# Precomputed weight sums in DRAM scratch, and gate products on VectorE, in a one-core block kernel

## The chip, the cores and the metric

One core of one Trainium2 chip runs the whole kernel. The metric is the device time of one execution in microseconds: 713.98 us is the median of three runs (713.1 to 714.77).

## The reference

One layer of a sequence model with x of 512 positions by 1024 features, all float32:

```python
h = rms_norm(x, norm_mix_g)
cb, cc, cin, q, k, v, f_logit, g_logit = split(h @ w_in)
y_conv = (cb * causal_dwconv(cc * cin, conv_mix_w)) @ w_out_conv
o = forgetting_attention(q, k, v, log_sigmoid(f_logit + b_f))     # 8 heads of 64, causal
y_attn = o @ w_out_attn
g_conv, g_attn = split(sigmoid(g_logit + b_gate))
x = x + (g_conv * y_conv + g_attn * y_attn) @ w_o
h = rms_norm(x, norm_ffn_g)
a, b = split(causal_dwconv(h @ w_up, conv_ffn_w))                 # 2 x 2816 wide
x = x + (silu(a) * b) @ w_down
return rms_norm(x, norm_f_g)
```

## The kernel before

Everything is kept transposed: 128 features on the partitions, 512 positions along a row. Every product is made of three matmuls. A float32 weight is split into a high part (`wh`, rounded to float32r by ScalarE) and a low part (`wl`, the rest, one subtraction on VectorE), the activations likewise, and high by high, low by high and high by low are summed in PSUM (`mm3`, in halves of 256 positions).

Weights stream from DRAM in chunks of 128 x 1024 in a fixed list `stream`. `load` issues the DMA of a chunk on SP's queue into a raw buffer, `split` makes `wh` and `wl` of it (two buffers each), `chunk` hands them to the matmuls. `load` runs up to `LOOK = 7` chunks ahead (`AHEAD = 3` during attention), as far as raw buffers are free.

The stages in order: v projection; attention, with the conv, q and k projections filled in between its heads (32 score units; each unit's softmax product `pp` is scaled on GpSimd and transposed three units later); the gate stage, j = 0 to 7, with for each j the two gates of a 128-feature block, then the chunk `mix` (y_conv into PSUM tile `yc`, y_attn into `ya`), then the merge into `mh` and `ml`; w_o (`wo`); up projection with 12 of 22 blocks (two `up` chunks each), first down projection, up projection of the other 10, second down projection; the last down blocks and the final norm.

Some products of 2 x 2 blocks are made with seven block products instead of eight: the gates of j = 3 to 7 (`gate_pair`) and most of the down projection (`down`). A step covers two such sets, and its weights are 14 blocks of 128 x 128: six plain ones (chunk `P`) and eight that are sums (chunk `F`). The table `wst` holds a step in DRAM. Two of four kinds of sum are made while loading: SP loads four blocks into the F buffer, GpSimd issues a second DMA that adds four blocks to them, then two GpSimd additions of 128 x 256 (L182 and L183, in `forms`) make the other four from these and P. P chunks and ordinary ones share four raw buffers, F chunks have four of their own (`NRAW`).

In `gate_pair`, VectorE assembles the two gates `a` (`ga`) and `b` (`gb`) from four PSUM banks, and GpSimd multiplies both by the norm factor `rb1` (L812, L813). ScalarE takes the sigmoid. VectorE multiplies by `yc` and `ya`, GpSimd adds the two (L850), ScalarE and VectorE split the sum.

For j = 1 and 2 the gates are ordinary products (PSUM tile `p_g`), and beside them x is loaded again in quarters (`xq`, DMAs on GpSimd's queue) and turned into the sums that the seven-product form needs (`x_forms`: tiles `tq`, `txh`, `txl`). In the up stage GpSimd multiplies silu(a) by b (`ge` for even j, `go` for odd j, the last of a phase on VectorE); `gh` and `gl` hold the split result for `down`, whose PSUM tiles are `dn`.

`keep` fixes an instruction's place on its engine; the rest is ordered by a scheduler. An engine's queue runs in order: what waits at its head holds all behind it.

Of the kernel before, what the change touches and what calls it, by code (L numbers as in the profile page):

```python
# [13 lines left out]
P = 128  # L14
# [9 lines left out]
EPS = 1e-6  # L24
AHEAD = 3
LOOK = 7
NRAW = {"raw": AHEAD + 1, "rf": 4}
NWARM = 7
NPP = 4
NCT = 5  # L30
# [30 lines left out]
def block_kernel(ctx, tc, xT, vecs, wv, win, wmix, wo, wup, wst, wdp, outT):  # L61
# [10 lines left out]
    def keep(ins):  # L72
        return tc.keep_in_program_order(ins)
# [38 lines left out]
    early = qk_i[0] + qk_i[1]  # L112
    late = conv_i[0] + qk_i[2] + conv_i[1] + qk_i[3] + conv_i[2] + conv_i[3] + [20, 28]

    def double(n):
# [25 lines left out]
    rfp = []  # L141
    later = []
    held = dict.fromkeys(NRAW, 0)
    stage = {"add": 0, "sum": 0}

    def after_split():

# [2 lines left out]
            st.enter_context(tc.issue_after(ins))  # L150
        return st

    def tag_of(k):
        return "rf" if stream[k][0][0] == "F" else "raw"

    def load(upto):
        for k in range(len(raws), min(upto, len(stream) - 1) + 1):
            nm, src, ncol = stream[k]
            tag = tag_of(k)
            if held[tag] == NRAW[tag] or tag == "rf" and not rfp:  # L160
                return
            held[tag] += 1
            raw = (rfp[0] if tag == "rf" else wp).tile([P, D], F32, tag=tag, name=f"raw_{nm}", bufs=NRAW[tag])
            if k == 0:

                keep(nc.scalar.dma_start(raw[:, :VW], src[:, :VW]))
                keep(nc.sync.dma_start(raw[:, VW:ncol], src[:, VW:]))
            elif tag == "rf":
                keep(nc.sync.dma_start(raw[:, : 4 * P], src[:, : 4 * P]))
# [7 lines left out]
    def forms(k):  # L177
        while stage["sum"] <= min(k + 3, stage["add"] - 1):
            a = stage["sum"]
            if tag_of(a) == "rf":  # L180
                f, p = (raws[x].rearrange("p (a b) -> p a b", b=P) for x in (a, a - 1))
                keep(nc.gpsimd.tensor_add(f[:, 4:6], f[:, 0:4:2], p[:, 1:6:3]))  # L182
                keep(nc.gpsimd.tensor_add(f[:, 6:8], f[:, 4:6], p[:, 2:6:3]))  # L183
            stage["sum"] += 1
        while stage["add"] < len(raws):
            a = stage["add"]
            if tag_of(a) == "rf":
                keep(nc.gpsimd.dma_start(raws[a][:, : 4 * P], stream[a][1][:, 4 * P :], accum_op=ALU.add))
            stage["add"] += 1

    def run_later(k, us):

# [17 lines left out]
    def split(hl=None):  # L210

        k = len(parts)
        if k == len(stream):
            return
        nm, _, ncol = stream[k]
        load(k + (LOOK if k >= gs0 else AHEAD))
        forms(k)
        if hl is None:
            hl = []
            for x in "hl":  # L220
                if k == 0:
                    wp.tile([P, PADW[x]], F32, tag=f"pad{x}", name=f"pad_{x}")
                hl.append(wp.tile([P, D], F32R, tag=f"w{x}", name=f"w{x}_{nm}", bufs=2)[:, :ncol])
        hi, lo = hl
        raw = raws[k]
        if k == 0:
            for cs in (slice(0, VW), slice(VW, S + H)):
                keep(nc.vector.tensor_copy(hi[:, cs], raw[:, cs]))
        else:
            ins = nc.scalar.activation(hi, raw, AF.Copy)  # L230
            order["hi"] = ins.ins
            if k < KB:
                keep(ins)
        ins = nc.vector.tensor_sub(lo, raw, hi.bitcast(F32))  # L234
        order["lo"] = ins.ins
        if k < KB:
            keep(ins)
        held[tag_of(k)] -= 1
        assert tag_of(k) == "raw" or stage["sum"] > k
        parts.append((hi, lo))  # L240
        run_later(k, {"u": 1.7, "P": 1.6, "F": 0.75}.get(nm[0], 3.5))

# [50 lines left out]
    )  # L293

    def place_of(f, s_):
        c = 3 * s_ + f if f < 3 else 2 * s_ + f - 3 if f < 5 else 4 + s_ + 2 * (f - 5)
        return slice(c * P, (c + 1) * P)

    def pair(ns, form, banks):
# [428 lines left out]
    for i in range(n + LA):  # L728
        if i < n:
            scores(*units[i])  # L730
        take = 1 if i < n + LA - 1 else len(fill)
# [14 lines left out]
    rfp.append(gxp)  # L746
# [76 lines left out]
    for j in range(KB):  # L823
        gs = []
        if j == 0:
            x_load(0)
            x_load(1)
            evac_gate(0, gs)(gp[0])
            evac_gate(8, gs)(gp[1])
        elif j < GS:  # L830
            for c, ev in enumerate((evac_gate(j, gs), evac_gate(8 + j, gs))):
                run_all(proj(20 + 8 * c + j, f"g{c}{j}", ev, acc))
                q = 2 * j - 2 + c
                x_forms(q)
# [12 lines left out]
        a, b = gs  # L847
        nc.vector.tensor_mul(a, a, yc)
        nc.vector.tensor_mul(b, b, ya)
        nc.gpsimd.tensor_add(a, a, b)  # L850
# [4 lines left out]
    rfp.clear()  # L855
# [68 lines left out]

    fp = ctx.enter_context(tc.tile_pool(name="fp", bufs=1))
    fp.tile([P, PADL], F32, tag="pad", name="pad_f")
    rfp.append(fp)

# [275 lines left out]
def _layout(i):  # L1204
# [41 lines left out]
    wup = blocks(i["w_up"][0])  # L1246
    wup = np.stack([wup[:NP], wup[NP:]], axis=1).reshape(2 * NP, P, D)
    wdn = blocks(i["w_down"][0]).reshape(KB, P, NP, P)
    wst = []
    for d in STEPS[0] + STEPS[1]:  # L1250
        def pick(*which):
            return [wdn[2 * i + m, :, 2 * q + k] for i, q in d for m, k in which]

        w = pick((1, 1), (0, 0), (0, 1)) + pick((1, 0), (1, 0)) + pick((1, 1), (0, 0))
        wst.append(np.concatenate(w, axis=1))
    for j in range(GS, KB):
        for d in range(2):
            w = []
            for which in (((1, 1), (0, 0), (0, 1)), None, ((1, 1), (0, 0))):
                for q in (2 * d, 2 * d + 1):  # L1260
                    for m, k in which or ((1, 0), (1, 0)):
                        w.append(win[20 + 8 * m + j][:, (2 * q + k) * P : (2 * q + k + 1) * P])
# [38 lines left out]
```

## Time and profile before

| | |
|---|---|
| median of three runs | 713.98 us (713.1 to 714.77) |
| profiled execution | 711.97 us, span 710.2 us |
| mean granted TensorE clock | 0.996 |
| GpSimd additions of 128 x 256 at L182 | 27, mean 1281 ns |
| low parts of F chunks (`wl_F`, L234) | 27, mean 1500 ns |
| low parts of up chunks (`wl_up`, L234) | 44, mean 1223 ns |
| DMAs on GpSimd's queue | 11.31 MB, 8.3% of 16 DMA engines over the span |
| DMAs on SP's queue | 70.65 MB, 31.7% |

The profile shows one execution on the chip. PE is TensorE's matmuls, PEld its weight loads, DVE is VectorE, ACT ScalarE, POOL GpSimd, SP the queue that issues most DMAs. A timeline row begins with its start and its duration in us; a name left of the arrow is the tile written, names right of it are read; in brackets stands how long the engine was idle before it, and what ended that. A row of waits has the waiting line, the awaited one, and then the total in us, the number of waits and the longest.

### The profile page before, as it was taken

Reading aid. Unit: us, or ns where it says so; the run is one execution under the profiler, and the core shown is the slowest. Engines: PE = TensorE matmul, PEld = TensorE weight load, DVE = VectorE, ACT = ScalarE, POOL = GpSimd, SP = SyncE. Lnnn points to the kernel's source line nnn. Section 1 sums busy time; section 2 is a strip of 40 time slices with the busy share of each in tenths; the row PEclk is TensorE's granted clock in tenths of the full one; section 3 lists DMA queues with packets and bytes.
Section 4 is the critical chain, followed back from the end, with each engine's and each line's share of the span. In section 5 each row is a group of like instructions: output and inputs, shape, how many; then the busy total and the mean of one; then the engine's idle time right before and its main releaser. Section 6 shows DMA issues by size and latency. Waiting matters only on the chain. (4 is left out here: it accounts for less than half of the span.)

```text
span 710.2 us, 14598 instructions
## 1 busy us (share of the span) xinstructions
PE 694.5 (98%) x6017; PEld 690.6 (97%) x6017; DVE 506.7 (71%) x772; ACT 340.4 (48%) x538; POOL 225.3 (32%) x234
## 2 busy tenths in 40 slices
PE   8999999999999999999999999999999999999995
PEld 8999999999999999999999999999999999999995
DVE  6677777766477788744377777779885678878953
ACT  6665645555465443344254444445443345444542
POOL 4124433322134677343301101136740110116202
PEclk9999999999999999999999999999999999999998
DMA  8513222222355655462323322357863332256303
GB/s 255 167 63 112 69 66 86 63 87 61 120 178 136 177 134 141 142 205 93 90 90 98 112 90 90 115 137 173 216 151 103 94 115 90 90 143 148 93 27 120
DMA packets 31491, 84.11 MB, mean 118 GB/s; under 512 B 3744, under 2 KB 6432, under 8 KB 31424
## 3 DMA queue, kind: packets, MB, share of 16 engines
q1 hardware_dynamic: 24736, 70.65, 31.7%
q0 software_dynamic: 5424, 11.31, 8.3%
q10 hardware_dynamic: 1264, 1.22, 0.5%
q8 instruction: 47, 0.77, 0.5%
q14 instruction: 20, 0.16, 0.1%
HBM read 81.00 MB, written 2.10 MB: 117 GB/s over the span
## 5 line engine op out<-in xcount | busy, mean ns | idle before, releaser
L264 PE MATMUL p_up<-x1h,wh_up 128*128 128x256 f32 x536 | 104.5, 276 | 0.0
L264 PE MATMUL p_up<-x1l,wh_up 128*128 128x256 f32 x536 | 104.4, 276 | 0.0
L264 PE MATMUL p_up<-x1h,wl_up 128*128 128x256 f32 x536 | 104.4, 276 | 0.0
L230 ACT ACTIVATE wh_up<-raw_up 128x1024 fp32r<-128x1024 f32 x44 | 46.7, 1060 | 89.1 <-PE p_up L264 68.8
L264 PEld LDWEIGHTS p_up<-x1h,wh_up 128*128 128x128 f32 x536 | 80.7, 188 | 0.0
L264 PEld LDWEIGHTS p_up<-x1l,wh_up 128*128 128x128 f32 x536 | 80.7, 188 | 0.0
L264 PEld LDWEIGHTS p_up<-x1h,wl_up 128*128 128x128 f32 x536 | 80.7, 188 | 0.0
L234 DVE TENSOR_TENSOR wl_up<-raw_up,wh_up 128x1024 fp32r<-128x1024 f32 x44 | 53.8, 1223 | 20.6 <-ACT wh_up L230 20.6
L264 PE MATMUL p_in<-xgh,wh_in 128*128 128x256 f32 x288 | 56.9, 279 | 1.0 <-ACT wh_in L230 1.0
L960 POOL TENSOR_TENSOR ge<-fu,fu 128x512 f32<-128x512 f32 x11 | 17.1, 1554 | 126.3 <-DVE fu L538 113.4
L264 PE MATMUL p_in<-xgh,wl_in 128*128 128x256 f32 x288 | 56.5, 277 | 0.0
L264 PE MATMUL p_in<-xgl,wh_in 128*128 128x256 f32 x288 | 56.4, 277 | 0.0
L230 ACT ACTIVATE wh_F<-raw_F 128x1024 fp32r<-128x1024 f32 x27 | 28.7, 1065 | 52.6 <-PE ya L264 24.7
L234 DVE TENSOR_TENSOR wl_F<-raw_F,wh_F 128x1024 fp32r<-128x1024 f32 x27 | 40.5, 1500 | 18.2 <-ACT wh_F L230 18.1
L947 DVE TENSOR_TENSOR fz<-p_up,rb_n 128x512 f32<-128x512 f32 x44 | 30.3, 690 | 30.1 <-PE p_up L264 30.1
L264 PEld LDWEIGHTS p_in<-xgh,wh_in 128*128 128x128 f32 x288 | 44.7, 188 | 1.9 <-ACT wh_in L230 1.2
L264 PEld LDWEIGHTS p_in<-xgl,wh_in 128*128 128x128 f32 x288 | 43.6, 188 | 0.0
L264 PEld LDWEIGHTS p_in<-xgh,wl_in 128*128 128x128 f32 x288 | 43.5, 188 | 0.0
L182 POOL TENSOR_TENSOR raw_F<-raw_F,raw_P 128x256 f32<-128x256 f32 x27 | 34.6, 1281 | 18.4 <-DMA raw_F<-in_wst_dram 18.4
L282 PE MATMUL p_up<-x1h,wh_up 128*128 128x256 f32 x168 | 40.3, 277 | 0.0
L282 PE MATMUL p_up<-x1l,wh_up 128*128 128x256 f32 x168 | 40.2, 276 | 0.0
L234 DVE TENSOR_TENSOR wl_in<-raw_in,wh_in 128x1024 fp32r<-128x1024 f32 x26 | 33.1, 1275 | 6.7 <-ACT wh_in L230 6.3
(309 smaller groups left out, 2119.4 us busy)
## 6 DMA issues: line engine op xcount, KB each, us to landing
raw_up<-in_wup_dram SPq DMA_DIRECT2D x44, 512.0 KB, 3.6
raw_in<-in_win_dram SPq DMA_DIRECT2D x26, 512.0 KB, 3.5
raw_P<-in_wst_dram SPq DMA_DIRECT2D x27, 384.0 KB, 3.6
raw_F<-in_wst_dram SPq DMA_DIRECT2D x27, 256.0 KB, 3.5
raw_F<-in_wst_dram POOLq DMA_DIRECT2D x27, 256.0 KB, 4.5
raw_mix<-in_wmix_dram SPq DMA_DIRECT2D x8, 512.0 KB, 4.1
raw_wo<-in_wo_dram SPq DMA_DIRECT2D x8, 512.0 KB, 3.6
xq<-in_xT_dram POOLq DMA_DIRECT2D x8, 256.0 KB, 3.9
```

Source lines behind the costliest of these rows:

```text
L182: keep(nc.gpsimd.tensor_add(f[:, 4:6], f[:, 0:4:2], p[:, 1:6:3]))
L230: ins = nc.scalar.activation(hi, raw, AF.Copy)
L234: ins = nc.vector.tensor_sub(lo, raw, hi.bitcast(F32))
L264: keep(nc.tensor.matmul(out[:, cs], w, x[:, cs], start=start and i == 0 and c == 0, stop=stop and i == 2 and c == len(cut) - 1,))
L282: keep(nc.tensor.matmul(out, wl if x == 1 else wh, xl if x == 2 else xh, start=opens and bk not in seen, stop=closes and bk not in left,))
L947: nc.vector.tensor_mul(z, p, rb2)
L960: keep(nc.gpsimd.tensor_mul(ge, a.rearrange(halves_of, h=2), b.rearrange(halves_of, h=2)))
```

## The change

The table `wst` keeps ten blocks a step. The sums of F are made in DRAM scratch (pool `dsp`, tiles `sum0` to `sum13`, two steps a tile, the last one step) by six DMAs a tile: copy four blocks, add four blocks; copy two of the sums on, add two blocks; copy those on, add two blocks. Copies go to SP's queue, adds (`accum_op`) to GpSimd's. The list `todo` holds all 84, two tiles' lists interleaved; `tick` issues the next one: once for each attention score unit, and afterwards at each split of an ordinary chunk (`in`, `mix`, `wo`, `up`) and of every second F. F is then loaded like any chunk, from the scratch. All chunks share five raw buffers; the F buffers and `forms` are gone.

The products with `rb1` and the sum of the two gated terms move to VectorE, for all eight j. The yc matmuls take all high parts of the weight first and its low part last. Nothing else of the arithmetic changes.

```diff
-NRAW = {"raw": AHEAD + 1, "rf": 4}
+NRAW = 5
+    def group(i):
+        ns = groups[i]
+        t = dsp.tile([P, len(ns), D], F32, tag=f"sum{i}", name=f"sum{i}")
...
+        return [
+            copy(f(0, 4), w(6, 10)),
+            add(f(0, 4), w(0, 4)),
+            copy(f(4, 6), f(0, 2)),
+            add(f(4, 6), w(2, 4)),
+            copy(f(6, 8), f(4, 6)),
+            add(f(6, 8), w(4, 6)),
+        ]
+    for i0, i1 in ((0, ngate), (ngate, len(groups))):
+        for i in range(i0, i1, 2):
+            todo += [op for ops in zip(*(group(x) for x in range(i, min(i + 2, i1)))) for op in ops]
+    def tick():
+        if todo:
+            todo.pop(0)()
     def double(n):
-        return [(f"P{n}", wst[n, :, : 6 * P], 6 * P), (f"F{n}", wst[n, :, 6 * P :], D)]
+        return [(f"P{n}", wst[n, :, : 6 * P], 6 * P), (f"F{n}", sums[n], D)]
...
-                keep(nc.gpsimd.tensor_add(f[:, 4:6], f[:, 0:4:2], p[:, 1:6:3]))
-                keep(nc.gpsimd.tensor_add(f[:, 6:8], f[:, 4:6], p[:, 2:6:3]))
...
-                keep(nc.gpsimd.dma_start(raws[a][:, : 4 * P], stream[a][1][:, 4 * P :], accum_op=ALU.add))
...
-        forms(k)
+        if k >= gs0 and (nm[0] in "imwu" or nm[0] == "F" and int(nm[1:]) % 2):
+            tick()
...
-            nc.gpsimd.tensor_mul(a, a, rb1)
-            nc.gpsimd.tensor_mul(b, b, rb1)
+            nc.vector.tensor_mul(a, a, rb1)
+            nc.vector.tensor_mul(b, b, rb1)
...
-        for pp, hh, ll, o in ((yc, ych, ycl, 0), (ya, oth, otl, 4)):
-            for k in range(4):
-                ks = slice((o + k) * P, (o + k + 1) * P)
-                mm3(pp, wh[:, ks], wl[:, ks], hh[:, k, :], ll[:, k, :], k == 0, k == 3)
+        passes([
+            (yc[:, cs], 0, wh[:, k * P : (k + 1) * P], wl[:, k * P : (k + 1) * P], ych[:, k, cs], ycl[:, k, cs],
+             True, True)
+            for k in range(4) for cs in halves
+        ], 8)
+        for k in range(4):
+            ks = slice((4 + k) * P, (5 + k) * P)
+            mm3(ya, wh[:, ks], wl[:, ks], oth[:, k, :], otl[:, k, :], k == 0, k == 3)
...
-        nc.gpsimd.tensor_add(a, a, b)
+        nc.vector.tensor_add(a, a, b)
```

How it stands on the engines. VectorE, one gate step (j = 5 there), from the assembly of the gates to the merged result's low part; before:

```order
L807 TENSOR_TENSOR gz_3337<-gs_3224,gz_3337 128x256
L808 TENSOR_TENSOR gb_3338<-gs_3222,gz_3337 128x512
L234 TENSOR_TENSOR wl_F_3403<-raw_F_3135,wh_F_3402 128x1024
L848 TENSOR_TENSOR ga_3336<-ga_3336,yc_3347 128x512
L849 TENSOR_TENSOR gb_3338<-gb_3338,ya_3348 128x512
L234 TENSOR_TENSOR wl_P_3460<-raw_P_3205,wh_P_3459 128x768
L234 TENSOR_TENSOR wl_F_3486<-raw_F_3207,wh_F_3485 128x1024
L852 TENSOR_TENSOR ml<-ga_3336,mh 128x512
L234 TENSOR_TENSOR wl_mix_3514<-raw_mix_3289,wh_mix_3513 128x1024
```

and now:

```order
L821 TENSOR_TENSOR gz_3561<-gs_3450,gz_3561 128x256
L826 TENSOR_TENSOR ga_3560<-ga_3560,rb_n_539 128x512
L822 TENSOR_TENSOR gb_3562<-gs_3448,gz_3561 128x512
L827 TENSOR_TENSOR gb_3562<-gb_3562,rb_n_539 128x512
L249 TENSOR_TENSOR wl_F_3625<-raw_F_3493,wh_F_3624 128x1024
L866 TENSOR_TENSOR ga_3560<-ga_3560,yc_3571 128x512
L867 TENSOR_TENSOR gb_3562<-gb_3562,ya_3572 128x512
L249 TENSOR_TENSOR wl_P_3684<-raw_P_3517,wh_P_3683 128x768
L868 TENSOR_TENSOR ga_3560<-ga_3560,gb_3562 128x512
L249 TENSOR_TENSOR wl_F_3708<-raw_F_3547,wh_F_3707 128x1024
```

Two products stand ahead of the first low part of F, and the sum ahead of the second one. The low part of mix still follows.

SP's queue at the end of the first up phase, where the chunks of the first down projection begin; before:

```order
L171 DMA raw_up_5794<-in_wup_dram 128x1024
L171 DMA raw_P_5855<-in_wst_dram 128x768
L169 DMA raw_F_5857<-in_wst_dram 128x512
L171 DMA raw_P_5926<-in_wst_dram 128x768
L169 DMA raw_F_5928<-in_wst_dram 128x512
L171 DMA raw_P_5996<-in_wst_dram 128x768
```

and now (`sum_97` is the scratch tile of the last step, the buffer numbers of the scratch being 84 to 97):

```order
L202 DMA raw_P_5859<-in_wst_dram 128x768
L202 DMA raw_F_5921<-sum_89 128x1024
L132 DMA sum_97<-in_wst_dram 128x512
L202 DMA raw_P_5990<-in_wst_dram 128x768
L202 DMA raw_F_6056<-sum_89 128x1024
L132 DMA sum_97<-sum_97 128x256
L202 DMA raw_P_6124<-in_wst_dram 128x768
```

Two copies stand between the loads; the second one needs the first add of this tile, and the third P stands behind it.

GpSimd's queue around that point, before (the accumulating load and the sums of the first steps, between the products of the up stage):

```order
L188 DMA raw_F_5857<-in_wst_dram 128x512
L960 TENSOR_TENSOR ge_5924<-fu_5851,fu_5919 128x512
L182 TENSOR_TENSOR raw_F_5857<-raw_F_5857,raw_P_5855 128x256
L183 TENSOR_TENSOR raw_F_5857<-raw_F_5857,raw_P_5855 128x256
L188 DMA raw_F_5928<-in_wst_dram 128x512
```

and now:

```order
L135 DMA sum_95<-in_wst_dram 256x1x256
L983 TENSOR_TENSOR go_5857<-fu_5786,fu_5852 128x512
L135 DMA sum_96<-in_wst_dram 256x1x256
L976 TENSOR_TENSOR ge_5988<-fu_5917,fu_5983 128x512
L135 DMA sum_97<-in_wst_dram 128x512
L135 DMA sum_97<-in_wst_dram 128x256 x2
```

The sums are gone, and the first add of `sum_97` stands behind the product `ge` of j = 10.

More of the change, by code (lines that the diff above doesn't have):

```diff
@@ L113, in block_kernel, with copy, add @@
     late = conv_i[0] + qk_i[2] + conv_i[1] + qk_i[3] + conv_i[2] + conv_i[3] + [20, 28]
+    dsp = ctx.enter_context(tc.tile_pool(name="dsp", bufs=1, space=bass.MemoryType.DRAM))
+    sums = {}
+    groups = [[NFF + 2 * j, NFF + 2 * j + 1] for j in range(KB - GS)]
+    ngate = len(groups)
+    groups += [list(range(n, min(n + 2, NFF))) for n in range(0, NFF, 2)]
+    todo = []
+    def group(i):
+        ns = groups[i]
+        t = dsp.tile([P, len(ns), D], F32, tag=f"sum{i}", name=f"sum{i}")
+        for k, n in enumerate(ns):
+            sums[n] = t[:, k, :]
+        w = wst[ns[0] : ns[-1] + 1].rearrange("n p c -> p n c")
+        w, f = ((lambda a, b, z=z: z[:, :, a * P : b * P]) for z in (w, t))
+        def copy(dst, src):
+            return lambda: keep(nc.sync.dma_start(dst, src))
+        def add(dst, src):
+            return lambda: keep(nc.gpsimd.dma_start(dst, src, accum_op=ALU.add))
+        return [
[12 more added lines that the diff above has]
+            todo.pop(0)()
     def double(n):
-        return [(f"P{n}", wst[n, :, : 6 * P], 6 * P), (f"F{n}", wst[n, :, 6 * P :], D)]
+        return [(f"P{n}", wst[n, :, : 6 * P], 6 * P), (f"F{n}", sums[n], D)]
     def gate_n(j):
@@ L140, in block_kernel @@
     raws, parts, order = [], [], {}
-    rfp = []
     later = []
-    held = dict.fromkeys(NRAW, 0)
-    stage = {"add": 0, "sum": 0}
+    held = [0]
     def after_split():
@@ L158, in load @@
             nm, src, ncol = stream[k]
-            tag = tag_of(k)
-            if held[tag] == NRAW[tag] or tag == "rf" and not rfp:
+            if held[0] == NRAW:
                 return
-            held[tag] += 1
-            raw = (rfp[0] if tag == "rf" else wp).tile([P, D], F32, tag=tag, name=f"raw_{nm}", bufs=NRAW[tag])
+            held[0] += 1
+            raw = wp.tile([P, D], F32, tag="raw", name=f"raw_{nm}", bufs=NRAW)
             if k == 0:
@@ L172, in load @@
             raws.append(raw[:, :ncol])
[L177 to L182, printed above, removed]
-                keep(nc.gpsimd.tensor_add(f[:, 6:8], f[:, 4:6], p[:, 2:6:3]))
[L184 to L189, printed above, removed]
     def run_later(k, us):
@@ L237, in split @@
             keep(ins)
-        held[tag_of(k)] -= 1
-        assert tag_of(k) == "raw" or stage["sum"] > k
+        held[0] -= 1
         parts.append((hi, lo))
@@ L295, in place_of @@
     def place_of(f, s_):
-        c = 3 * s_ + f if f < 3 else 2 * s_ + f - 3 if f < 5 else 4 + s_ + 2 * (f - 5)
+        c = 2 * (f % 3 if f < 6 else 3) + s_
         return slice(c * P, (c + 1) * P)
@@ L730, in block_kernel @@
             scores(*units[i])
+            tick()
         take = 1 if i < n + LA - 1 else len(fill)
@@ L854, in block_kernel @@
     gx.close()
-    rfp.clear()
     xp = ctx.enter_context(tc.tile_pool(name="xp", bufs=1, side="right"))
@@ L1248, in _layout @@
     wdn = blocks(i["w_down"][0]).reshape(KB, P, NP, P)
+    order = ((1, 1), (0, 0), (0, 1), (1, 0), (1, 0))
     wst = []
     for d in STEPS[0] + STEPS[1]:
[L1251 to L1255, printed above, removed]
+        wst.append(np.concatenate([wdn[2 * i + m, :, 2 * q + k] for m, k in order for i, q in d], axis=1))
     for j in range(GS, KB):
         for d in range(2):
[L1258 to L1262, printed above, removed]
+            w = [
+                win[20 + 8 * m + j][:, (2 * q + k) * P : (2 * q + k + 1) * P]
+                for m, k in order for q in (2 * d, 2 * d + 1)
+            ]
             wst.append(np.concatenate(w, axis=1))
```

6 lines of the change are left out of this document (removed).

## The prediction

> **What bounds the kernel now.** I read the head of the page first, then busy time in windows of 10 us over the whole span, then the waits of TensorE alone, then the timeline around each of those waits.
>
> ```profile
> span 710.2 us, 14598 instructions
> PE 694.5 (98%) x6017; PEld 690.6 (97%) x6017; DVE 506.7 (71%) x772; ACT 340.4 (48%) x538; POOL 225.3 (32%) x234
> ```
>
> TensorE works 98% of the span, and the change leaves it the same matmuls. So only its idle 710.2 - 694.5 = 15.7 us can be won. The windows tell where that lies (after the window's length: PE, PEld, DVE, ACT, POOL, clock, DMA share, GB/s):
>
> ```profile
> 190.00:200.00 10.00, 8.26 (x71) 7.86 (x70) 7.40 (x12) 8.75 (x11) 2.36 (x3) 1.00 0.36 129
> 210.00:220.00 10.00, 8.92 (x76) 8.53 (x75) 7.24 (x10) 5.77 (x7) 3.87 (x5) 1.00 0.51 140
> 260.00:270.00 10.00, 9.28 (x82) 9.09 (x81) 9.90 (x11) 3.54 (x5) 7.70 (x5) 1.00 0.54 151
> 280.00:290.00 10.00, 9.28 (x81) 9.09 (x81) 7.13 (x9) 3.30 (x5) 6.63 (x5) 1.00 0.33 113
> 290.00:300.00 10.00, 10.00 (x91) 10.00 (x90) 8.12 (x11) 4.88 (x7) 1.94 (x1) 1.00 0.36 109
> 650.00:660.00 10.00, 9.65 (x83) 9.28 (x82) 9.97 (x11) 6.36 (x9) 7.73 (x8) 1.00 0.72 159
> 660.00:670.00 10.00, 9.34 (x80) 9.14 (x79) 8.89 (x12) 3.82 (x5) 1.07 (x1) 1.00 0.28 80
> ```
>
> A window without a hole holds 90 or 91 matmuls (290 to 300). The holes before the last 10 us that the change can reach lie in the gate stage (four windows, 4.3 us) and at the second down projection (1.0 us). The waits of TensorE give them names:
>
> ```profile
> PE p_g L264 <- DVE wl_in L234: 2.3, 2, 1.7
> PE yc L264 <- DVE wl_mix L234: 2.0, 3, 0.7
> PE dn L282 <- DVE gl L987: 0.7, 1, 0.7
> PE dn L282 <- DVE wl_F L234: 0.3, 1, 0.3
> ```
>
> 5.3 us in all, each behind VectorE, none behind a DMA. That is the most this change can win; the rest is the start and the tail, which it does not touch.
>
> **Why VectorE is late there.** In the last gate steps, timeline of VectorE, GpSimd and TensorE:
>
> ```profile
> 277.08 2.31 DVE L234 TENSOR_TENSOR wl_F<-raw_F,wh_F 128x1024 fp32r<-128x1024 f32 x1
> 280.47 1.76 DVE L234 TENSOR_TENSOR wl_mix<-raw_mix,wh_mix 128x1024 fp32r<-128x1024 f32 x1
> 282.15 1.48 DVE L234 TENSOR_TENSOR wl_P<-raw_P,wh_P 128x768 fp32r<-128x768 f32 x1
> 281.11 1.71 POOL L182 TENSOR_TENSOR raw_F<-raw_F,raw_P 128x256 f32<-128x256 f32 x1
> 288.97 1.23 DVE L234 TENSOR_TENSOR wl_F<-raw_F,wh_F 128x1024 fp32r<-128x1024 f32 x1 [2.76 <-ACT wh_F L230]
> 290.72 0.68 DVE L849 TENSOR_TENSOR gb<-gb,ya 128x512 f32<-128x512 f32 x1
> 291.31 0.95 DVE L234 TENSOR_TENSOR wl_P<-raw_P,wh_P 128x768 fp32r<-128x768 f32 x1
> 266.29 0.51 PE L264 MATMUL yc<-ych,wl_mix 128*128 128x256 f32 x2 [0.72 <-DVE wl_mix L234]
> 282.28 0.51 PE L264 MATMUL yc<-ych,wl_mix 128*128 128x256 f32 x2 [0.72 <-DVE wl_mix L234]
> ```
>
> The same low-part subtraction of 128x1024 takes 1.23 us when GpSimd is idle (288.97) and 1.76 to 2.31 us while GpSimd adds; 128x768 takes 0.95 against 1.48. So GpSimd's sums, though off the path, set VectorE's speed. The two PE rows also show the period of a gate step: 16.0 us for five weight chunks.
>
> **The change, part by part.**
>
> *Sums leave GpSimd.* 54 additions and 27 accumulating loads go. In one gate step VectorE gets back, on the rows above alone, 1.08 + 0.53 + 0.53 = 2.1 us. It takes over two products and one sum of 128x512, by the 0.68 row 3 x 0.68 = 2.0 us. In sum that is even, but the order matters: only the sum (0.68) stands ahead of the low part of mix, while wl_F (1.08 shorter) and wl_mix (0.53 shorter) stand ahead of its end. So wl_mix ends about 0.9 us earlier.
>
> *The yc matmuls in another order.* The first use of the low part moves from the third matmul to the seventeenth, some 14 x 0.11 us = 1.5 us later (10 us over 91 matmuls). Either edit alone covers 0.72; the wait on yc goes whole: 2.0 us. Bounds: nothing, if VectorE came 1.5 us later than now; 2.0 at most.
>
> *p_g, first wait.*
>
> ```profile
> 193.25 1.04 ACT L230 ACTIVATE wh_in<-raw_in 128x1024 fp32r<-128x1024 f32 x1
> 193.38 0.69 DVE L849 TENSOR_TENSOR g<-g,ya 128x512 f32<-128x512 f32 x1
> 194.15 1.27 POOL L850 TENSOR_TENSOR g<-g,g 128x512 f32<-128x512 f32 x1 [5.16 <-DVE g L849]
> 194.32 2.17 DVE L234 TENSOR_TENSOR wl_in<-raw_in,wh_in 128x1024 fp32r<-128x1024 f32 x1 [0.26 <-ACT wh_in L230]
> 196.55 0.51 PE L264 MATMUL p_g<-xgh,wl_in 128*128 128x256 f32 x2 [1.70 <-DVE wl_in L234]
> ```
>
> The sum of j = 0 runs on GpSimd beside wl_in, which takes 2.17. Now it stands on VectorE ahead of wl_in: 194.07 + 0.69 = 194.76, then 1.23 gives 196.0 instead of 196.5. I take 0.5 won of 1.7. Bounds: 0.5 won; 0.4 lost if wl_in kept its 2.17.
>
> *p_g, second wait.*
>
> ```profile
> 204.40 0.93 POOL L188 DMA_DIRECT2D raw_F<-in_wst_dram  x1 [6.13 <-DMA raw_F<-in_wst_dram]
> 210.74 0.72 ACT L768 ACTIVATE xq<-xq,vec 128x512 f32<-128x512 f32 x1 [3.45 <-DMA xq<-in_xT_dram]
> 213.73 0.51 PE L264 MATMUL p_g<-xgh,wl_in 128*128 128x256 f32 x2 [0.56 <-DVE wl_in L234]
> ```
>
> GpSimd is held 6.13 us by the accumulating load, the x load behind it leaves late, ScalarE waits 3.45 us for it, and wh_in and wl_in stand behind. The accumulating load is gone. An add into `sum_89` now stands ahead of that x load, but its copy is issued some chunks earlier on SP. I take the 0.56 as won (0 at worst).
>
> *dn.*
>
> ```profile
> 658.23 1.71 POOL L182 TENSOR_TENSOR raw_F<-raw_F,raw_P 128x256 f32<-128x256 f32 x1
> 661.83 1.28 DVE L987 TENSOR_TENSOR gl<-go,gh 128x512 fp32r<-128x512 f32 x2
> 662.56 0.39 PE L282 MATMUL dn<-gl,wh_P 128*128 128x256 f32 x1 [0.66 <-DVE gl L987]
> ```
>
> VectorE is 9.97 of 10 us busy ahead of it, beside GpSimd sums like the 1.71 row. With 0.5 to 1.1 us less for each of the weight subtractions in that stretch both waits go: 1.0 us won (0 at worst).
>
> *The new transfers.* 84 of them: 42 copies on SP, 42 adds on GpSimd. TensorE is not touched by them unless a queue is held so long that a weight is late. On GpSimd they stand among the softmax products:
>
> ```profile
> 186.76 2.23 POOL L763 DMA_DIRECT2D xq<-in_xT_dram  x4 [14.29 <-PE yc L264]
> 101.12 0.59 POOL L593 TENSOR_SCALAR pp<-pp,m 128x384 f32<-128x384 f32 x1 [2.91 <-DVE m L592]
> 112.04 0.49 PE L609 MATMUL tp<-ident,pp 128*128 128x128 f32 x3
> ```
>
> An issue takes 2.23 / 4 = 0.56 us for 128 rows, at most double for 256. A product that ends at 101.71 is transposed at 112.04: 10 us of cover against 1.1 us. Cost 0. On SP a copy waits for an add to land, and every weight load behind it waits too. Tiles go in pairs with two ticks between dependent transfers, each the time of a weight chunk (an up chunk is 48 matmuls, 5.3 us). `sum_97`, one step alone, has one tick between them, at the end of the first up phase: the tightest place:
>
> ```profile
> 472.33 1.60 POOL L960 TENSOR_TENSOR ge<-fu,fu 128x512 f32<-128x512 f32 x1 [8.99 <-DVE fu L538]
> raw_F<-in_wst_dram POOLq DMA_DIRECT2D x27, 256.0 KB, 4.5
> raw_P<-in_wst_dram SPq DMA_DIRECT2D x27, 384.0 KB, 3.6
> 488.45 0.28 PE L282 MATMUL dn<-gh,wh_P 128*128 128x256 f32 x1
> ```
>
> The add stands behind ge of j = 10, which ends at 473.93. If it lands as an accumulating load does now, 4.5 us, SP gets on at 478.4, the load of the third P lands at 478.4 + 1.1 for two issues (0.56 each) + 3.6 = 483.1, and its high part, an estimated 0.95 by VectorE's row for that shape, is due at 488.45. Spare: 4.4 us. So the add may take 8.9 us before TensorE waits. No row shows an add into DRAM; 4.5 is the nearest row and I take it. Bounds 3.6 (a plain load) to three times 4.5, 13.5, since the add reads and writes memory instead of SBUF; the upper end costs 13.5 - 8.9 = 4.6 us.
> [...]
>
> *Fewer buffers.* Five for all chunks, where P and F had four each. A buffer comes back five chunks ahead, a 16.0 us gate step; less a split (1.0 + 1.2) and a landing (3.6) some 10 us are left. Cost 0; the cover is that distance.
>
> **The sum.** 2.0 + 0.5 + 0.56 + 1.0 = 4.1 us off the profiled execution's 711.97 (span 710.2 and 1.8 around it): 707.9. That execution lies 2.0 us below the median of the runs, 713.98, so for the median I forecast 713.98 - 4.1 = 709.9.
>
> **The rivals.**
>
> 1. *All of it goes*, the first wait on p_g too, as ScalarE and VectorE run ahead: 713.98 - 5.3 = 708.7. Against it: wh_in ends at 194.29 whatever happens, and 1.0 us of low part must follow. Chance 0.17.
> 2. *The waits move.* VectorE's 2.0 us of new work per step cancels what it gets back (it is 9.90 busy in 260 to 270), and only what the yc order hides is kept, or a held SP gives back 3 to 4 us. Won 0 to 1.4: 713.3. For it: the sums are even, as above. Chance 0.12.
> 3. *Slower: SP held by the add into `sum_97`.* If that add takes L us, TensorE waits L - 8.9. At L = 13.0 the gain is gone; from 14.4 on the kernel is slower by over 0.2%; at L = 20, 11.1 - 4.1 = 7.0 gives 721.0. For it: the copy, the add and the next copy each wait for a landing in memory. Against it: 4.5 us now. Chance 0.10. [...]
>
> **How the numbers follow.** Forecast 0.61, rivals 0.17, 0.12, 0.10. About 0.2%, 1.4 us, can be told from no change. Faster: 0.61 + 0.17 = 0.78; same 0.12; slower 0.10. The range starts at rival 1 less the runs' own spread of 0.8 us, 707.9, and reaches rival 2, 713.3; beyond it lie rival 3 and the outer tails. The forecast's own range is 708.7 to 711.5.
>
> **What would show it.** Right: no wait of yc on wl_mix; wl_F and wl_mix near 1.23 us; p_g waits of about 1.2 us in all; no GpSimd compute in the gate stage; DMA share higher in the attention stage with TensorE full there. Wrong: a wait of TensorE on wh_P or wh_F at 480 to 490 with SP behind a copy of sum_97; adds landing after 10 us and more; low parts still at 1.7 to 2.3 us, which would mean that it was not GpSimd's arithmetic that slowed them.

## The result, and the profile after

The changed kernel takes 705.31 us (median of four runs, 704.73 to 707.72), the kernel before on the same chip 713.54 us (712.51 to 714.77): ratio 0.989, interval 0.9861 to 0.9919. That is 8.2 us less, twice the forecast 4.1, and below the low end of the range, 707.9. The profiled execution is the slowest of the four, 707.72 us. Head of its page, then its waits of TensorE:

```profile
span 706.0 us, 14566 instructions
PE 694.1 (98%) x6017; PEld 692.2 (98%) x6017; DVE 494.1 (70%) x790; ACT 340.2 (48%) x538; POOL 155.8 (22%) x177
```

```profile
PE p_g L278 <- DVE wl_in L249: 1.1, 1, 1.1
PE tp L623 <- DVE ptl L627: 0.6, 1, 0.6
PE p_g L278 <- ACT wh_in L245: 0.6, 1, 0.6
```

No yc and no dn wait is left. GpSimd is busy 155.8 us instead of 225.3. A wait on `tp`, in attention, is new. Windows of 10 us at the places shown of before (PE, PEld, DVE, ACT, POOL, clock, DMA share, GB/s):

```profile
190.00:200.00 10.00, 8.23 (x63) 7.84 (x62) 5.97 (x11) 8.03 (x11) 1.71 (x3) 0.92 0.39 117
200.00:210.00 10.00, 10.00 (x82) 10.00 (x82) 7.88 (x13) 6.03 (x8) 2.70 (x4) 0.91 1.00 270
210.00:220.00 10.00, 10.00 (x90) 10.00 (x90) 9.07 (x14) 5.89 (x7) 1.05 (x1) 1.00 0.36 111
260.00:270.00 10.00, 10.00 (x90) 10.00 (x89) 8.36 (x13) 3.94 (x5) 0.00 (x0) 1.00 1.04 295
280.00:290.00 10.00, 10.00 (x91) 10.00 (x90) 7.13 (x12) 4.20 (x6) 2.42 (x3) 1.00 0.83 217
650.00:660.00 10.00, 10.00 (x91) 10.00 (x90) 7.93 (x13) 6.17 (x9) 0.00 (x0) 1.00 0.71 215
660.00:670.00 10.00, 10.00 (x91) 10.00 (x90) 8.78 (x13) 5.88 (x9) 0.00 (x0) 1.00 0.54 157
```

Behind the hole near 196 the clock column falls to 0.92 and 0.91: the record shows one stretch of 3.41 us at half speed, from 198.4, which costs half its length, 1.7 us. It is in this trace alone of the two taken of the changed kernel.

The low parts and transfers (groups by line with their shape; then DMA issues with KB and median us to landing):

```profile
L249 DVE TENSOR_TENSOR wl_F<-raw_F,wh_F 128x1024 fp32r<-128x1024 f32 x27 | 33.0, 1224 | 16.6 <-ACT wh_F L245 16.6
L249 DVE TENSOR_TENSOR wl_mix<-raw_mix,wh_mix 128x1024 fp32r<-128x1024 f32 x8 | 9.8, 1225 | 4.2 <-ACT wh_mix L245 4.2
sum<-in_wst_dram POOLq DMA_DIRECT2D x27, 256.0 KB, 5.1
sum<-in_wst_dram POOLq DMA_DIRECT2D x13, 512.0 KB, 7.3
```

VectorE's subtractions of these chunks all run at 1.21 to 1.23 us, against a mean of 1500 ns before for wl_F; of all its subtractions of 128x1024 one, a `wl_in` in the attention stage (near 54 us), still takes 1.65. An add into DRAM lands in 5.1 to 7.3 us; 4.5 was taken.

### The profile page after: what moved, and what is told of

The parts are those of the page before. It is cut to its first block, busy times and chain, and to the rows that moved or that the text cites. A ratio compares the mean times of both kernels' runs of the same rounds, so it can differ in the third digit from the quotient of the medians.

```text
span 706.0 us, 14566 instructions
## 1 busy us (share of the span) xinstructions
PE 694.1 (98%) x6017; PEld 692.2 (98%) x6017; DVE 494.1 (70%) x790; ACT 340.2 (48%) x538; POOL 155.8 (22%) x177
## 3 DMA queue, kind: packets, MB, share of 16 engines
q10 hardware_dynamic: 1264, 1.22, 0.5%
## 4 chain that ended last, share of the span: by engine, by line
PE 92%; DMA 3%; DVE 1%; ACT 1%; issue 1%; POOL 1%; DVEq 0%; POOLq 0%; ACTq 0%
PE p_up L278 26%; PE dn L296 11%; PE p_in L278 10%; PE p_up L296 8%; PE gs L296 7%; PE p_wo L278 6%; PE yc L296 3%; PE ya L278 3%; PE p_g L278 3%; PE pd L278 2%; PE pa L457 2%; DMA sum<-in_wst_dram 2%; PE pb L459 2%; PE p_q L278 2%; PE p_k L278 2%; PE o L638 1%
## 5 line engine op out<-in xcount | busy, mean ns | idle before, releaser
L135 POOL DMA_DIRECT2D sum<-in_wst_dram x42 | 44.9, 1080 | 108.6 <-DMA sum<-sum 79.2
L249 DVE TENSOR_TENSOR wl_F<-raw_F,wh_F 128x1024 fp32r<-128x1024 f32 x27 | 33.0, 1224 | 16.6 <-ACT wh_F L245 16.6
```

Of the source, the lines that this page charges most:

```text
L135: return lambda: keep(nc.gpsimd.dma_start(dst, src, accum_op=ALU.add))
```

## Where the time went: a ledger by stages

The waits name holes but do not add up to the gain. Both programs issue the same 6017 matmuls, so I subtract the start of the matmul of the same number in two traces and list how the difference grows from stage to stage (us; minus is gained on the first trace of before). The matmuls at the ends of the stages start in that trace at 187.6, 205.8, 225.7, 293.8, 485.2, 545.1, 641.4 and 680.9 us; the stages left out change by 0.03 at most.

| kernel | up to the gate stage | j = 0 and first half of j = 1 | rest of j = 1, and j = 2 | j = 3 to 7 | first down | second down | all |
|---|---|---|---|---|---|---|---|
| before, second trace | +0.06 | -0.07 | +2.53 | -0.03 | +0.16 | +0.01 | +2.66 |
| after, first trace | +1.07 | +1.64 | -1.78 | -2.35 | -0.71 | -2.13 | -4.24 |
| after, second trace | +1.20 | -0.56 | -1.78 | -2.35 | -0.71 | -2.13 | -6.33 |
| sums in DRAM alone | +2.91 | -0.13 | -1.78 | -2.35 | -0.71 | -2.13 | -4.16 |
| products on VectorE alone | +0.42 | -0.39 | -0.78 | -1.12 | +0.18 | -0.23 | -1.90 |
| yc order alone | -0.19 | -0.04 | -0.13 | +0.69 | +0.03 | -0.29 | +0.05 |
| products and yc order | +0.89 | -0.71 | -0.85 | -2.35 | -0.03 | -0.20 | -3.21 |
| no accumulating loads | +0.12 | +0.15 | +0.27 | -1.92 | -0.71 | -2.13 | -4.21 |
| no additions on GpSimd | +0.41 | +1.63 | +0.78 | -2.35 | -0.71 | -2.13 | -2.37 |
| all tiles in pairs | +0.64 | -0.73 | -1.78 | -2.35 | -0.71 | -2.13 | -7.10 |
| no transfers | +0.29 | -0.85 | -1.78 | -2.35 | -0.71 | -2.13 | -7.50 |
| pairs, split ahead | -0.03 | -2.31 | -1.78 | -2.35 | -0.71 | -2.13 | -9.29 |
| x on SP's queue | +0.63 | +0.15 | -1.12 | +0.19 | -0.02 | 0.00 | -0.16 |

The start of the program (up to matmul 40) is in the first column and varies from -0.3 to +2.0 us from execution to execution; for the sums alone it is +1.97.

## The experiments

Every kernel was timed beside runs of the kernel before, whose medians were 714.44 us for the first four below, 714.21 for products with yc order, no transfers, pairs and before itself, 713.7 for the two halves of the sums and the last version, and 714.53 for the x loads.

### The change again, and its three parts alone

The change again, as it is:

> The changed kernel once more, unaltered. Theory A (waits, and the clock behind them): the profile of before had no half-clock window before the tail and the profile of after had one of 3.41 us, which costs 1.7 us, and the two differ by 4.2 us; the medians differ by 8.2 us because most runs of before have such windows and most runs of after have none. Then a run of after without such a window has a mean granted clock of 0.996 to 0.997 and takes 704.5 to 706 us, and each window lowers the mean clock by 0.0024 and adds 1.7 us. Theory B (TensorE itself became faster beside the new traffic): runs of equal clock differ by 8 us between before and after, and matmuls in a window with no hole number more than 91 per 10 us.

Measured: 705.2 us (705.15 to 705.62), 9.2 us off 714.44; ratio 0.9874 (0.9857 to 0.9891). Theory A's 704.5 to 706 us holds. There is no stretch at half speed in this trace, and windows without a hole list 90 or 91 matmuls as before, which speaks against theory B. These four runs lie within 0.5 us (the first four, one of them with the half-speed stretch, within 3.0), those of the kernel before beside them between 712.39 and 716.78.

Sums in DRAM alone (products and yc order as before):

```diff
-            nc.vector.tensor_mul(a, a, rb1)
+            nc.gpsimd.tensor_mul(a, a, rb1)
...
-        passes([
...
+        for pp, hh, ll, o in ((yc, ych, ycl, 0), (ya, oth, otl, 4)):
```

> The DRAM sums and the five shared buffers alone; gate products and their sum stay on GpSimd, yc keeps its old order. Theory A: the waits of dn (2.7 us in the trace, both phases together) go, since GpSimd no longer adds weights; of yc's 2.0 us most go; the first wait on p_g (1.7) stays, because the sum of j = 0 still runs on GpSimd beside wl_in: about 709.5 us. Rival (VectorE's own arithmetic is what matters): the gate stage stays as before and only dn's 2.7 us are won: 711.

Measured: 706.49 us (705.93 to 708.6), ratio 0.9897 (0.9879 to 0.9914): 7.9 us off, by far the largest part, and 3.0 us more than theory A had. It wins the whole of the yc and dn stages by itself. The first hole of p_g stays at 1.7 us, since GpSimd still adds beside `wl_in`.

Products on VectorE alone:

```diff
-            nc.gpsimd.tensor_mul(a, a, rb1)
+            nc.vector.tensor_mul(a, a, rb1)
...
-        nc.gpsimd.tensor_add(a, a, b)
+        nc.vector.tensor_add(a, a, b)
```

> The gate products and their sum on VectorE alone; weight sums stay on GpSimd. Theory A: nothing or a loss, since GpSimd goes on adding weights beside VectorE and VectorE has 2.0 us more a gate step: 713 to 716 us. Rival: a gain of 1 us or more, because the shorter chain from gate to merged result is what counts: 712 us or less.

Measured: 710.47 us (709.79 to 712.04), ratio 0.9951 (0.9934 to 0.9967): 4.0 us off. The rival's number was right, theory A's wrong. VectorE loses less by the three operations than it wins when they are gone from GpSimd: the mean of wl_F falls from 1500 to 1328 ns. Whether the rival's own reason, the shorter chain, has a share was not tested. The yc wait falls from 2.0 to 0.4 us, the dn waits stay:

```profile
PE yc L264 <- DVE wl_mix L234: 0.4, 1, 0.4
PE dn L282 <- DVE wl_F L234: 0.8, 2, 0.4
```

The yc order alone:

```diff
-        for pp, hh, ll, o in ((yc, ych, ycl, 0), (ya, oth, otl, 4)):
...
+        passes([
...
+        for k in range(4):
```

> The order of the yc matmuls alone. Theory A: the three waits on wl_mix go, 2.0 us, and nothing else: 711.5 us. Rival (the wait moves to the next low part, wl_P or wl_F): no gain, 713.5 us.

Measured: 713.35 us (711.45 to 715.66), ratio 0.9986 (0.9971 to 1.0): 1.1 us off, not clear of noise, since the interval reaches 1.0, and near the rival's 713.5. The yc wait is gone, and a wait of the next step has its place, of almost the same size:

```profile
PE gs L282 <- DVE wl_F L234: 1.9, 3, 0.7
```

These holes lie at 244.6, 260.5 and 276.6 us, at the first wl_F of a gate step. TensorE comes there sooner, but VectorE is also later than before: this subtraction takes 3.13 to 3.36 us, where it took 1.43 to 2.10, because GpSimd's gate products now end some 1.4 us later, and in both traces it ends 1.10 us after them (see the last section). One step of the first trace of before:

```profile
256.40 1.61 POOL L813 TENSOR_TENSOR gb<-gb,rb_n 128x512 f32<-128x512 f32 x1
257.01 2.10 DVE L234 TENSOR_TENSOR wl_F<-raw_F,wh_F 128x1024 fp32r<-128x1024 f32 x1 [2.74 <-ACT wh_F L230]
```

and here:

```profile
257.81 1.58 POOL L813 TENSOR_TENSOR gb<-gb,rb_n 128x512 f32<-128x512 f32 x1
257.24 3.25 DVE L234 TENSOR_TENSOR wl_F<-raw_F,wh_F 128x1024 fp32r<-128x1024 f32 x1 [1.62 <-ACT wh_F L230]
```

Why GpSimd is later was not followed up. So the prediction's "either edit alone covers 0.72" holds for the wait on yc, but the order alone hardly won any time.

Products and yc order together, sums as before:

```diff
-            nc.gpsimd.tensor_mul(a, a, rb1)
+            nc.vector.tensor_mul(a, a, rb1)
...
+        passes([
```

> The kernel before, with the gate products on VectorE and the new yc order; the sums still made while loading, GpSimd's additions of 128x256 kept. Theory A (the sums' additions on GpSimd beside VectorE are what costs; V alone already took the yc waits): 3.9 to 4.5 us off the kernel before, 710.0 us. Rival (the edits add: 4.0 + 1.1 = 5.1 us off): 709.3 us. Rival 2 (the late weight of the next step that Y alone met comes back): 711.5 us or more.

Measured: 708.34 us (707.97 to 709.57), ratio 0.9919 (0.9902 to 0.9937): 5.9 us off, more than the 5.1 of the two alone. With the products gone from GpSimd, the subtraction that took 3.25 us in the yc order alone takes 1.22 (at 256.04), and the order wins the rest of j = 3 to 7: the ledger's -2.35, against -1.12 for the products alone. What the sums win on top is 9.2 - 5.9 = 3.3 us, nearly the two down stages, 0.71 + 2.13 = 2.84.

### Which part of the sums

No accumulating loads (the addend left out of the sums, GpSimd's additions kept):

```diff
-                keep(nc.gpsimd.dma_start(raws[a][:, : 4 * P], stream[a][1][:, 4 * P :], accum_op=ALU.add))
+                pass
```

> The kernel before without its 27 accumulating loads; F's first four blocks stay plain, GpSimd's additions stay, the addend is left out of the sums. Theory A (an accumulating load that lands late holds GpSimd's queue, the x load of the gate step behind it leaves late, and the second hole of p_g with the half-speed window behind it varies with that): the hole of 0.6 to 2 us near 213 us goes, the spread of the runs falls from 4 us to about 1 us, the median 2 to 3 us off the kernel before (711.5 us), the yc and dn waits stay. Rival (the additions alone matter): 714 us with the same spread.

No additions (those four blocks left as loaded):

```diff
-                keep(nc.gpsimd.tensor_add(f[:, 4:6], f[:, 0:4:2], p[:, 1:6:3]))
-                keep(nc.gpsimd.tensor_add(f[:, 6:8], f[:, 4:6], p[:, 2:6:3]))
...
-                keep(nc.sync.dma_start(raw[:, : 4 * P], src[:, : 4 * P]))
+                keep(nc.sync.dma_start(raw[:, : 8 * P], src[:, : 8 * P]))
```

> The kernel before without GpSimd's 54 additions of 128x256; SP loads all eight blocks of F instead of four (512 KB for 256 KB), the accumulating loads stay, the four blocks that the additions made are left as loaded. Theory A (the additions slow VectorE's subtractions from 1.23 us to 1.8 to 2.3 us, which makes the yc and dn holes): no yc wait, no dn wait, wl_F near 1.23 us; 2.3 us in the gate steps and 2.5 us in the down stages come back, 4.8 us off, 709.4 us, the spread of the runs staying at 3 to 4 us with the hole of p_g near 213 us. Rival (VectorE is late for its own work, as where the products stand on it): the waits stay at half or more, 712 us or more.

Measured: 707.96 us (707.58 to 709.07), ratio 0.9917 (0.9901 to 0.9933), and 709.45 us (708.28 to 711.49), ratio 0.9939 (0.9919 to 0.9959). The second came as expected, but for 0.6 us of yc wait at j = 2. In the first the hole of p_g near 213 is gone and the runs lie within 1.5 us, near what its theory A had. But it won 5.7 us, not 2 to 3: it too clears the down stages whole and leaves yc waiting at j = 2 alone (0.5 and 0.9 us), though GpSimd adds as long as ever. Its groups:

```profile
L234 DVE TENSOR_TENSOR wl_F<-raw_F,wh_F 128x1024 fp32r<-128x1024 f32 x27 | 38.0, 1408 | 20.9 <-ACT wh_F L230 20.9
L182 POOL TENSOR_TENSOR raw_F<-raw_F,raw_P 128x256 f32<-128x256 f32 x27 | 36.1, 1336 | 15.2 <-DMA raw_F<-in_wst_dram 9.3 <-DVE wl_F L234 3.8 <-DVE fu L538 2.2
```

So both halves are needed for the holes in the down stages. The traces fit this account: the accumulating load holds GpSimd, and the additions and products behind it then fall late, beside the subtractions that TensorE waits for. At the second down projection before, GpSimd waits 3.44 us for such a load (until 647.89), and its last addition ends at 661.1; without the loads it ends at 652.0. The theory of slow subtractions alone, on record with the run, was too small. The two gains, 5.7 and 4.3, add up to more than the 7.9 of the sums in DRAM: they share the same holes. Two things stay open there. ScalarE, too, waits 2.62 us for a late addition (`wh_F` at 650.51 in the first trace of before), and the runs do not separate a late high part from a late low part. Nor do they show whether the late addition or the late `ge` and `go` count more.

### What the transfers cost

No transfers (F loaded from plain blocks, its sums left out):

```diff
-        return [(f"P{n}", wst[n, :, : 6 * P], 6 * P), (f"F{n}", sums[n], D)]
+        return [(f"P{n}", wst[n, :, : 6 * P], 6 * P), (f"F{n}", wst[n, :, 2 * P :], D)]
...
-        if todo:
-            todo.pop(0)()
+        todo.clear()
```

> The kernel after, without its 84 transfers: F is loaded from plain blocks of the table, so the eight sums of each step are left out; the loads keep their number and size. Theory A (the transfers cost one thing, the chain of the single gate tile that holds GpSimd in the attention stage, 0.9 us by the two traces): 704.3 us, and the wait of the transpose on the attention tile is gone, the rest of the trace as in after. Rival (the transfers cost nothing, as predicted; the 0.9 is another thing): 705.2 us. Rival 2 (the transfers also slow the weight loads or the copies in the feed-forward stage): 703.5 us or less.

Tiles in pairs over the whole list:

```diff
-    for i0, i1 in ((0, ngate), (ngate, len(groups))):
-        for i in range(i0, i1, 2):
-            todo += [op for ops in zip(*(group(x) for x in range(i, min(i + 2, i1)))) for op in ops]
+    for i in range(0, len(groups), 2):
+        todo += [op for ops in zip(group(i), group(i + 1)) for op in ops]
```

> The kernel after, with the scratch tiles paired over the whole list (14 tiles, 7 pairs): the last gate tile takes turns with the first feed-forward tile, and the last step's tile with the one before it, so every transfer has two ticks to the one that needs it. Theory A (the sum of the single gate tile held GpSimd for 6.36 us because one tick is shorter than copy and landing): the wait of 0.7 us on the transpose goes, the attention stage comes back by 0.9 us, 704.3 us. Rival (another hold takes its place, the adds landing after 5 to 7 us as a rule): 705.2 us.

Measured: 703.95 us (703.87 to 704.05), ratio 0.9856 (0.9837 to 0.9874), and 704.55 us (704.42 to 704.85), ratio 0.9865 (0.9846 to 0.9883). So the 84 transfers cost about 1.25 us (705.2 - 703.95), between the 0.9 of theory A and the 1.7 of rival 2, and the pairs get back 0.65 of that. The `tp` wait is gone in both. GpSimd's timeline in the changed kernel shows why:

```profile
167.49 1.05 POOL L135 DMA_DIRECT2D sum<-in_wst_dram  x1 [6.36 <-DMA sum<-sum]
169.36 1.17 POOL L607 TENSOR_SCALAR pp<-pp,m 128x512 f32<-128x512 f32 x1
```

Besides `sum_97` the last gate tile, `sum_88`, is alone on the list. Its add waits 6.36 us for the copy issued one tick earlier, and the softmax products `pp` stand behind it. In the pairs no add of that stretch waits. Between the pairs and no transfers 0.6 us is left; the ledgers differ by 0.35 at the start and 0.12 at j = 0, which I do not attribute.

### Why the runs won more than the traces

From trace to trace the change wins 6.33 us, from median to median 8.2 and 9.2. The kernel before was run again for a second trace:

> The kernel before, unchanged, for a second trace. Theory A (its usual execution loses 2 to 3 us more than the one profiled at first, by half-speed windows of TensorE of 3.4 us, 1.7 us each, or a late start of the full clock): the trace shows one or two such windows or a start of the clock after 8 us, at a mean clock of 0.994. Rival (the waits themselves vary, with the landing of the accumulating loads): no such window, a clock of 0.996 or more, and waits of p_g, yc and dn that sum to 6 to 8 us instead of 5.3.

Measured: 714.19 us (712.96 to 716.97), ratio 1.0006 (0.9993 to 1.002). The profiled execution took 714.63 us, close to the median, 2.66 us more than the first one. 2.53 of it lie at one place, the rest of j = 1 and j = 2. Its waits of TensorE, then its window there (the first trace had 76 matmuls at clock 1.00):

```profile
PE p_g L264 <- DVE wl_in L234: 2.5, 2, 1.7
PE yc L264 <- DVE wl_mix L234: 1.5, 2, 0.8
PE p_g L264 <- ACT wh_in L230: 1.4, 1, 1.4
```

```profile
210.00:220.00 10.00, 7.85 (x52) 7.45 (x52) 4.97 (x8) 5.32 (x7) 2.92 (x4) 0.83 0.53 154
```

Its timeline at the place:

```profile
204.49 0.93 POOL L188 DMA_DIRECT2D raw_F<-in_wst_dram  x1 [6.22 <-DMA raw_F<-in_wst_dram]
212.60 0.72 ACT L768 ACTIVATE xq<-xq,vec 128x512 f32<-128x512 f32 x1 [5.31 <-DMA xq<-in_xT_dram]
214.32 0.50 PE L264 MATMUL p_g<-xgh,wh_in 128*128 128x256 f32 x2 [1.39 <-ACT wh_in L230]
215.58 0.79 PE L264 MATMUL p_g<-xgh,wl_in 128*128 128x256 f32 x2 [0.76 <-DVE wl_in L234]
```

The x load behind the accumulating load lands 1.9 us later than in the first trace (212.60 against 210.74), the hole of 0.56 becomes 1.39 + 0.76, and from 215.6 TensorE has half its clock for 3.41 us. The theory's half-speed stretch and the rival's longer wait are both there. To test the wait by itself, only the last two pairs of x loads were put on SP's queue:

```diff
-            nc.gpsimd.dma_start(x, xT[:, 2 * q + i, :])
+            (nc.sync if q > 1 else nc.gpsimd).dma_start(x, xT[:, 2 * q + i, :])
```

> The kernel before, with the last two pairs of x loads (q = 2 and 3) on SP's queue instead of GpSimd's, nothing else. There they no longer stand behind the accumulating load into raw_F, which held GpSimd for 6.13 us in one trace of the kernel before and 6.22 us in the other, with x landing at 210.7 and 212.6 us. Theory A (that hold is the second hole of p_g, 0.6 us in one trace, 2.2 us and a half-speed window of 1.7 us in the other, and so the greater part of what the usual execution loses beyond the first trace): x lands before 208 us, no hole of p_g near 213 us, no half-speed window there, 0.9 us off the first trace of the kernel before and 2 to 3 us off the median of its runs, 711.5 us. Rival (what moves the runs lies elsewhere): within 1 us of the kernel before, 713.5 us.

Measured: 712.0 us (711.53 to 713.48), ratio 0.9969 (0.9957 to 0.9981): 2.5 us off, as theory A had it. GpSimd is held still, but nothing that TensorE needs stands behind:

```profile
205.19 0.70 ACT L768 ACTIVATE xq<-xq,vec 128x512 f32<-128x512 f32 x1
205.39 0.94 POOL L188 DMA_DIRECT2D raw_F<-in_wst_dram  x1 [9.18 <-DMA raw_F<-in_wst_dram]
```

Against the first trace of before it wins 0.16 us (in the ledger 1.12 at the place, but 0.63 is lost at the start), against the median 2.5: a comparison of whole times with a single good trace would have called the edit worthless. Its twelve runs fall in two groups: seven at a mean clock of 0.996 or 0.997, median 711.75 us, and five at 0.993 or 0.994, median 713.16. The difference of 1.4 us is near one half-speed stretch, 1.7. Among the 74 runs of the kernel before beside the experiments the clock separates the times less (58 at 0.995 or less, median 714.43; 16 above, 713.84), so how often these have the stretch, and how often only a long wait, stays open.

### A version that beats both

The pairs, with the split of the second input chunk of j = 1 issued ahead of j = 0's sigmoids and merge:

```diff
+            if idx % 8:
                 nc.scalar.activation(g, g, AF.Sigmoid, bias=col(BG + idx))
...
+        if j == 0:
+            while len(parts) < chunk.n + 2:
+                split()
...
+        with after_split() if j == 0 else ExitStack():
+            for g, idx in zip((a, b), (0, 8)) if j == 0 else ():
+                nc.scalar.activation(g, g, AF.Sigmoid, bias=col(BG + idx))
             nc.vector.tensor_mul(a, a, yc)
             nc.vector.tensor_mul(b, b, ya)
             nc.vector.tensor_add(a, a, b)
```

> The pairs version, with the split of the second input chunk of j = 1 issued ahead of the sigmoids, the gated products and their sum of j = 0. Theory A (the last hole of the gate stage, 1.1 us of p_g behind wl_in near 196 us and 0.2 us behind wh_in, is only the order on ScalarE and VectorE): both go, 1.3 to 1.5 us off the pairs version, 703.1 us. Rival (the merge of j = 0 ends later and the low part of mix or the next inputs wait for VectorE instead): 704.5 us.

Measured: 702.83 us (702.68 to 703.1), ratio 0.9845 (0.9825 to 0.9864): 10.9 us off the kernel before, 1.7 off the pairs, as theory A had it. `wl_in` is done at 192.8, against 197.6 in the first trace of the changed kernel (1.1 us of this is the earlier stages), and p_g has no wait left. The changed kernel, then this one:

```profile
196.37 1.22 DVE L249 TENSOR_TENSOR wl_in<-raw_in,wh_in 128x1024 fp32r<-128x1024 f32 x1
191.56 1.23 DVE L248 TENSOR_TENSOR wl_in<-raw_in,wh_in 128x1024 fp32r<-128x1024 f32 x1 [0.53 <-ACT wh_in L244]
```

## Why the prediction was wrong, point by point

**Direction and mechanism: right in the main.** The waits on yc and dn went, wl_F and wl_mix came to 1.224 and 1.225 us, and the sums leaving GpSimd alone bring 7.9 us. Rival 3 did not happen: the copy behind the add into `sum_97` is issued 4.4 us after the add (472.45 to 476.83), against an estimated 4.5 and a limit of 8.9:

```profile
472.45 0.84 POOL L135 DMA_DIRECT2D sum<-in_wst_dram  x1
476.83 0.48 SPq L132 DMA_DIRECT2D sum<-sum  x1
```

One reading under the mechanism was off. The wl_F of 2.31 us at 277.08, whose 1.08 us were booked to the sums, ends 1.08 us after the gate sum on GpSimd, which the other edit moves (278.31 to 279.39):

```profile
276.38 1.93 POOL L850 TENSOR_TENSOR ga<-ga,gb 128x512 f32<-128x512 f32 x1 [1.22 <-DVE gb L849]
```

With the sums in DRAM alone, where the gate sum stays on GpSimd, five wl_F still take 1.67 to 2.08 us.

**"5.3 us ... is the most this change can win": wrong, the step that failed first.** It took the waits' listed lengths for the time lost. The windows that I had quoted say more. The chain of the second trace of after gives the full rate:

```profile
475.28 57.12 PE dn L296 x504
```

57.12 / 504 = 0.113 us a matmul. A full window lists 90 or 91. The six windows with holes list 71, 76, 82, 81, 83 and 80, so 70 too few in all: 7.9 us, not the 5.3 of busy shares and waits. The ledger of the kernel without any of these holes has 0.71 + 2.13 + 2.35 + 1.78 + 2.31 = 9.28, which takes in places outside the six windows; 1.75 of that is the part of the first p_g hole that the change leaves. The reason for the difference: the matmul behind a hole of yc starts 0.99 us after its predecessor where 0.72 is listed, and the next one 0.22 after that, twice the usual step: 0.99 us lost. At the second down projection three holes are on the weight loads, 0.55, 0.17 and 0.86 us, of which the list of waits had two:

```profile
654.36 1.01 PEld L282 LDWEIGHTS dn<-gh,wl_F 128*128 128x128 f32 x8 [0.55 <-DVE wl_F L234]
659.40 1.00 PEld L282 LDWEIGHTS dn<-gh,wl_F 128*128 128x128 f32 x8 [0.17 <-DVE wl_F L234]
662.56 0.19 PEld L282 LDWEIGHTS dn<-gl,wh_P 128*128 128x128 f32 x1 [0.86 <-DVE gl L987]
```

The first down projection has two more, which the list of waits lacks and the prediction left at nothing:

```profile
487.40 1.01 PEld L282 LDWEIGHTS dn<-gh,wl_F 128*128 128x128 f32 x8 [0.21 <-DVE wl_F L234]
490.06 0.77 PEld L282 LDWEIGHTS dn<-gh,wl_P 128*128 128x128 f32 x6 [0.27 <-DVE wl_P L234]
```

**The terms.** dn 1.0: measured 2.84, of which 0.71 at the first down projection. yc 2.0 and the second p_g 0.56, together 2.56: measured 1.78 + 2.35 = 4.13. The first p_g 0.5: measured 0.56. In sum 7.53 against 4.1, on the same execution.

**"Cost 0" for the transfers: wrong by about 1.** The issue was priced at double 0.56 (1.05 measured), but not the wait ahead of it. I looked for the tile without a partner at the end of the list and named `sum_97`; `sum_88` is the same case in attention. Measured against the profiled execution: 7.53 - 1.05 in attention - 0.15 at the start = 6.33.

**"For the median I forecast 713.98 - 4.1": wrong.** The 2.0 us between the profiled execution and the median were kept as if they belonged to any kernel. In the second trace they are the second p_g hole, grown, and moving two pairs of x loads takes 2.5 us off the median. With these 2.0 us the account closes: 6.3 + 2.0 = 8.3, against 8.2 measured.

**Right in part.** "In sum that is even" for VectorE: from j = 3 to 7 it is busy 52.6 of 68.1 us before and 50.5 of 65.7 in the second trace of after. Fewer buffers: no wait of the changed kernel points to one.

## What to carry to other kernels

Count instructions per window on a bound engine: here missing matmuls times the time of one came near what the holes cost (7.9 us in six windows), while the list of waits left out a part (5.3). A profiled execution below the median of its runs may hold the best case of some wait; here that was the wait on a landing transfer, and the edit that removed it won more than the trace showed. Here, reordering the engine that waited only brought a wait of the same size at the next step; once the late engine had time, the order paid.

## What was not expected of the hardware

- Stretches of 3.41 us in which TensorE has half its clock, right behind holes. In the first trace of after (clock 0.50 from 198.37 to 201.78) the holes are of 0.62 and 1.14 us, in the second trace of before of 1.39 and 0.76 (clock 0.83 in the window from 210 to 220), without the additions one of 1.7 alone. In the 3.41 us just ahead of each, TensorE was idle 1.77, 2.15 and 1.78 us, by its modelled busy time. But behind the same 1.7 in both traces of before there is none: in the first one no 3.41 us between the start of the full clock and 690 us hold more than 1.74 us of idle time, and the window from 190 to 200 is at clock 1.00. Near its end, at 704.38, the clock fell to 0.50 after less, 1.28 us idle in the 3.41 us ahead, and so it did in the first trace of after, at 700.13. So in these traces neither the length of a hole nor the idle time just ahead settles alone whether the clock falls; what does stays open.
- The subtraction of 128x1024 takes 1.22 us where GpSimd rests, and up to 3.36 us where it works (yc order alone). It is not slowed evenly: its end follows the end of an operation of GpSimd by nearly the same time. The `wl_mix` of 280.47 + 1.76 = 282.23 us that the prediction shows ends 1.09 us after this addition (280.07 + 1.07 = 281.14):

```profile
280.07 1.07 POOL L183 TENSOR_TENSOR raw_F<-raw_F,raw_P 128x256 f32<-128x256 f32 x1
```

So it is in all fourteen traces: each of the 131 weight subtractions of 128x1024 (in, mix and F) that took over 1.3 us ended 1.07 to 1.10 us after the end of a GpSimd operation (18 of them in the first trace of before, the `wl_in` of 1.65 us in the first trace of after). So what a subtraction lost in these traces, between 0.1 and 2.1 us, depended on when GpSimd's operation ended, and was not a share of its own length.
